# Halving the raw weight tiles and doubling the width of their splits in a two-block transformer kernel

## The chip, the core and the metric

The kernel runs on one core of a Trainium2 chip. Its time is the device time of one execution in microseconds (us), from the first to the last instruction. Six names are used for the engines: PE is TensorE's matrix products, PEld its loads of stationary operands, DVE is VectorE, ACT is ScalarE, POOL is GpSimd, and SP is SyncE, which here does nothing but issue transfers. An engine takes its instructions strictly in the order in which the build has placed them; an instruction that waits holds up all that stand behind it on that engine.

## What is computed

The reference takes 256 tokens of width 1024 through two blocks in float32. Cut to what matters here:

```
x = x + concat(mla, fox, chunk attention) @ w_o       # block 1
x = x + cross attention over a memory of 256 tokens
x = x + (silu(h @ w_gate) * (h @ w_up)) @ w_down
for l in 0, 1:                                        # block 2
    x = x + gate_l * mixer_l(norm(x) * (1 + s_l) + b_l)
    h = norm(x) * (1 + s'_l) + b'_l
    16 experts of 16384 for each head and token (8 heads), by top-k of two lists of 128 keys
    x = x + gate'_l * sum over the chosen experts of softmax gate * gelu(u_e . h) * v_e
```

The modulation rows s, b and gate are themselves products of a vector of 1024 with a matrix of 1024 x 12288. The sum over experts is computed densely: the kernel forms gelu(u . h) for all 16384 experts and all 256 tokens, multiplies by a map G of gates that is zero wherever an expert was not chosen, and multiplies that by all of v. So u and v (64 MB each, for each of two layers) stream through the core once.

## The kernel before, in words

Every product with a weight matrix keeps float32 accuracy by splitting both operands into two float32r parts, high and low, and summing three products: high by high, high by low, low by high. For weights the split is done on the fly, by two operations for each piece: ACT copies the raw weights to `wh` in float32r (L281), and DVE subtracts it from the raw weights to give `wl` (L282). A raw weight tile is 128 x 2048 floats, 1 MB, loaded by one transfer on SP's queue (`load_w`, L274, and L1574 for v) into a ring `wraw` of 3 tiles. The split tiles are 128 x 512, in a ring of 5 for `wh` and 5 for `wl`. So each raw tile is split by four pairs of operations.

Four helpers use these tiles. `feat` (L324) makes 256 features of (h @ W) transposed, with 48 products of 256 columns for each raw tile (L298 to L300). `proj` (L339) makes 512 columns of h @ W token-major (L287 to L291). `wide_mm` (L372) multiplies a chunk of 128 rows with all 1024 columns (L379), and `wide_end` (L381) does the last two chunks of such a sum.

Each layer of block 2 passes over the experts twice. The first pass runs `feat` over u for 64 pairs of expert rows and writes gelu(u . h) to DRAM (`act`). The second pass runs `wide_mm` over v, also for 64 pairs: for pair n, `gated(n)` reads `act` back (L1523, into a tile `k2` of a ring of 5 that also holds its product), multiplies it by the map of gates on DVE (L1525), and splits the product into the high part on ACT (L1532) and the low part on DVE (L1533). Then two calls of `wide_mm` give 24 products of 512 columns.

In the second pass of layer 0 another stream runs beside it: the modulation of the other layer. For most pairs SP also loads 512 KB of its matrix (L435) and DVE multiplies and sums it in one operation of 128 x 1024 (L436). In layer 1 nothing runs beside the second pass.

The order of instructions on each engine is set at build time by a scheduler that weighs priorities and readiness; the order of rings and waits follows from it. On SP's queue the loads of v, of the modulation's matrix and of `act` stand in one line, so a load that waits for a buffer holds up the ones behind it.

Of the kernel before, what the change touches and what calls it, by code (L numbers as in the profile page):

```python
# [19 lines left out]
P = 128  # L20
# [13 lines left out]
# the candidate pairs of two descending lists of 16: rows from..to, columns, place of the first  # L34
# [6 lines left out]
# the reciprocal root's first guess, its first step y (C - x y^2) K, and what weighs its second  # L41
# [4 lines left out]
# columns of the per-partition constants, in the order kernel() lays them out  # L46
# [12 lines left out]
# shape-only constants: name -> width of its [128, width] block  # L59
# [14 lines left out]
def body(tc, A, out, dbg=None, stop=None):  # L74
# [17 lines left out]
    wp = pool("wraw", 3)  # L92
    sp = pool("split", 5)
# [81 lines left out]
    def inv_rms(dst, s0, s1, e=D * EPS):  # L175
        """dst [128, 1] = 1/sqrt((s0 + s1 + e) / 1024) (each [128, 1])."""
# [5 lines left out]
    def inv_rms_w(dst, s0, width):  # L182
        """dst [128, 1] = 1/sqrt(s0 / width + EPS)."""
# [5 lines left out]
    def diag(r):  # L189
        """[128, 128] with r [128, 1] on the diagonal: a transpose through it scales its rows."""  # L190
# [4 lines left out]
    def hl_tiles(kc, pl=None, name="hl"):  # L195
        """feature-major operand [128, kc, 256] as exact float32r parts, in pieces of 4 chunks."""
# [13 lines left out]
    def split_psum(hl, k, src, gain=None, bias=None, scale=None):  # L210
        """chunk(s) k of hl from src (PSUM [128, n, 256]); per-partition gain/bias columns."""
# [24 lines left out]
    def to_T(src, kc, hl, gain=None, bias=None, by=None, ks=None):  # L236
        """src(t, k) -> [128 tok, 128] AP; transposed (with rows scaled by the diagonals by[t]), scaled and split into hl."""
# [32 lines left out]
    def load_w(dram, off, per, ada=True):  # L270
        """one raw weight tile: [128, per] floats, contiguous by partition."""
        ada_tick(ada)
        w = wp.tile([P, 2048], F32, name="w")
        nc.sync.dma_start(w[:, :per], dap(dram, off, [[per, P], [1, per]]))  # L274
        return w

    def split_w(src, n):
        """float32r parts of src [128, n <= 512]."""
        h = sp.tile([P, 512], F32R, name="wh")
        l = sp.tile([P, 512], F32R, name="wl")  # L280
        ada_p["act"] = nc.scalar.activation(h[:, :n], src, AF.Copy).ins.name  # L281
        i_ = nc.vector.tensor_sub(l[:, :n], src, h[:, :n].bitcast(F32))  # L282
        ada_p["after"] = i_.ins.name
# [11 lines left out]
    def mmT(ps, hl, k, wh, wl, start, stop):  # L295
        """ps [features, 256] += W[k]^T @ chunk k of hl"""
# [5 lines left out]
    # work that runs beside a stream of weights, in portions between its pieces  # L302
# [33 lines left out]
    def proj(hl, kc, dram, off, n, evac, base=0, quiet=0, turn=None):  # L336
        """[256 tok, n <= 512] = hl^T @ W, W at dram[off] as pieces [128, 4 chunks, n]."""
# [9 lines left out]
        for k in order:  # L347
            m = min(4, kc - k)
            w = load_w(dram, off + k * P * n, m * n, len(order) - order.index(k) > quiet)
            j = 0  # L350
            while j < m:
                # the last two chunks tile by tile, so that the first tile's end comes early
                final = k == order[-1]
                js = [j, j + 1] if final and j == m - 2 else [j]
                if final and turn:
                    js = [turn[i] for i in js]
                ws = [split_w(w[:, q * n:(q + 1) * n], n) for q in js]
                last = None
                for t in range(2):
                    sl = slice(t * P, (t + 1) * P)  # L360
                    for q, (wh, wl) in zip(js, ws):
                        h_, l_ = pick(base + k + q, sl)
                        i_ = mm3(ps[t][:, :n], h_, l_, wh[:, :n], wl[:, :n], k == order[0] and j == 0 and q == js[0],
                                 final and j + len(js) == m and q == js[-1], after=last)
                        last = i_.ins.name if len(js) == 2 else None
                    if final and j + len(js) == m:
                        evac(t, ps[t][:, :n])
                for _ in js:
                    tick()
                j += len(js)  # L370

    def wide_mm(ps, w, i, lhs_of, first, last):  # L372
        """ps[t, half] += lhs_of(t)^T @ w[:, i*1024...]"""
        wh, wl = zip(*(split_w(w[:, i * 1024 + hf * 512:i * 1024 + (hf + 1) * 512], 512) for hf in range(2)))
        for t in range(2):
            h, l = lhs_of(t)
            for lhs, ww in ((h, wh), (h, wl), (l, wh)):
                for hf in range(2):
                    nc.tensor.matmul(ps[t, hf], lhs, ww[hf], start=first and lhs is h and ww is wh, stop=last and lhs is l)  # L379

    def wide_end(ps, w, lhs_of, evac):  # L381
        """the last pair of chunks, tile by tile and half by half"""
        ws = [[split_w(w[:, i * 1024 + hf * 512:i * 1024 + (hf + 1) * 512], 512) for i in range(2)] for hf in range(2)]
        last = None
        for t in range(2):
            for hf in range(2):
                for i in range(2):
                    last = mm3(ps[t, hf], *lhs_of(i, t), *ws[hf][i], False, i == 1, after=last).ins.name
# [1384 lines left out]
```

## Time and profile before

| what | value |
|---|---|
| time, median of 3 runs | 2292.16 us (2290.60 to 2295.77) |
| span of the profiled execution, first to last instruction | 2295.8 us |
| the slowest of the three runs, which agrees with that span | 2295.77 us |
| PE busy | 2259.0 us, 98% |
| DVE busy | 1753.4 us, 76% |
| ACT busy | 1274.5 us, 56% |
| transfers, mean over the span | 219 GB/s |

The profiled execution has nothing around its span that the times would add: its span equals the time of the slowest run. It lies 3.6 us above the median.

Busy time of PE is to be read with care: products are pipelined, and a product that is shown for 390 ns may follow the one before after 226 ns. How fast PE goes is therefore read from the number of products in a stretch, not from its busy share.

### The profile page before, as it was taken

What the parts mean: (1) busy time and instruction counts of PE and PEld (TensorE: products, weight loads), DVE (VectorE), ACT (ScalarE), POOL (GpSimd) and SP (SyncE); (2) the same over time, 40 slices, a digit from 0 to 9 for tenths busy, and PEclk for the clock granted to TensorE, in tenths of its full rate; (3) what the DMA queues carried; (4) which work ended last, traced back from release to release, by engine and by line L of the source; (5) the groups of instructions that cost most, each with busy time, mean ns of one, the idle gap of its engine ahead of it and who ended that gap; (6) DMA issues with size and microseconds to landing.
All of it is one profiled execution on the core that took longest, in us unless ns stands there. A gap on an engine that the chain in (4) does not pass through costs nothing.

```text
span 2295.8 us, 40651 instructions
## 1 busy us (share of the span) xinstructions
PE 2259.0 (98%) x15032; PEld 2053.3 (89%) x15032; DVE 1753.4 (76%) x4239; ACT 1274.5 (56%) x2324; POOL 20.6 (1%) x28
## 2 busy tenths in 40 slices
PE   8999999999999999999999999999999999999998
PEld 7889988899999999887778877999999999888886
DVE  7778887798767675688888888896767665777776
ACT  7656555455455555555555565555555555555554
POOL 0000000000000000000000020000000000000000
PEclk9999999999999999999999999999999999999999
DMA  6256786446655555889889533456555557666664
GB/s 249 97 183 249 275 317 236 168 166 234 212 180 175 183 183 185 289 313 322 318 314 325 209 129 134 169 207 222 192 184 174 175 181 248 252 252 237 245 245 145
DMA packets 107161, 503.59 MB, mean 219 GB/s; under 512 B 12369, under 2 KB 13521, under 8 KB 61650
## 3 DMA queue, kind: packets, MB, share of 16 engines
q1 hardware_dynamic: 87954, 465.19, 57.9%
q10 hardware_dynamic: 18720, 33.72, 3.9%
q8 instruction: 117, 1.92, 0.3%
q0 software_dynamic: 288, 2.10, 0.2%
q14 instruction: 82, 0.67, 0.1%
HBM read 464.25 MB, written 36.70 MB: 218 GB/s over the span
## 4 chain that ended last, share of the span: by engine, by line
PE 85%; DVE 7%; DMA 5%; ACT 1%; issue 1%; DVEq 0%; SPq 0%; ACTq 0%
PE acc L379 21%; PE acc L298 14%; PE acc L299 14%; PE acc L300 14%; DMA k<-act 5%; PE acc L287 4%; PE acc L290 3%; PE acc L291 3%; DVE wl L282 3%; PE mm L1491 3%; PE mm L1492 3%; DVE G L436 1%; PE pt L246 1%; PE pt L300 1%; PE pt L299 1%
## 5 line engine op out<-in xcount | busy, mean ns | idle before, releaser
L281 ACT ACTIVATE wh<-w 128x512 fp32r<-128x512 f32 (+1 forms) x1408 | 882.2, 630 | 847.7 <-PE acc L299 383.9
L282 DVE TENSOR_TENSOR wl<-w,wh 128x512 fp32r<-128x512 f32 (+1 forms) x1408 | 954.7, 689 | 283.1 <-ACT wh L281 275.2
L298 PE MATMUL acc<-q,wh 128*128 128x256 f32 x2592 | 745.2, 288 | 0.7 <-ACT q L223 0.7
L299 PE MATMUL acc<-q,wh 128*128 128x256 f32 x2592 | 733.2, 283 | 0.5 <-DVE q L224 0.5
L300 PE MATMUL acc<-q,wl 128*128 128x256 f32 x2592 | 729.8, 283 | 1.2 <-DVE wl L282 1.2
L379 PE MATMUL acc<-wh,q 128*128 128x512 f32 x1984 | 612.1, 390 | 0.0
L298 PEld LDWEIGHTS acc<-q,wh 128*128 128x128 f32 x2592 | 497.9, 192 | 1.5 <-ACT q L223 0.9
L299 PEld LDWEIGHTS acc<-q,wh 128*128 128x128 f32 x2592 | 497.2, 192 | 0.8 <-DVE q L224 0.7
L300 PEld LDWEIGHTS acc<-q,wl 128*128 128x128 f32 x2592 | 495.7, 192 | 1.4 <-DVE wl L282 1.4
L379 PEld LDWEIGHTS acc<-wh,q 128*128 128x128 f32 x1984 | 373.0, 188 | 77.1
L379 PE MATMUL acc<-wl,q 128*128 128x512 f32 x992 | 388.1, 393 | 7.0 <-DVE wl L282 6.7
L379 PEld LDWEIGHTS acc<-wl,q 128*128 128x128 f32 x992 | 186.6, 188 | 52.3 <-DVE wl L282 14.1
L1478 DVE TENSOR_TENSOR ohe<-iota,ijh 128x512 f16<-128x512 f16 x128 | 54.1, 425 | 121.3 <-PE mm L1492 121.3
L1525 DVE SCALAR_TENSOR_TENSOR k<-k,G 128x512 f32<-128x512 f32 x128 | 88.2, 689 | 65.2 <-DMA k<-act 63.8
L1492 PE MATMUL mm<-ohe,k 128*128 128x128 f16 x512 | 128.0, 297 | 0.0
L1491 PE MATMUL mm<-k 128*128 128x128 f16 x512 | 126.6, 293 | 0.0
L1493 ACT ACTIVATE G<-mm 128x512 f32<-128x512 f32 x128 | 76.5, 598 | 38.0 <-PE mm L1492 38.0
L290 PE MATMUL acc<-wl,q 128*128 128x512 f32 (+1 forms) x224 | 89.8, 402 | 0.0
L291 PE MATMUL acc<-wh,q 128*128 128x512 f32 (+1 forms) x224 | 87.1, 397 | 0.0
L1533 DVE TENSOR_TENSOR q<-k,q 128x512 fp32r<-128x512 f32 x126 | 86.2, 684 | 0.7
L287 PE MATMUL acc<-wh,q 128*128 128x512 f32 (+1 forms) x224 | 85.3, 402 | 0.0
L1532 ACT ACTIVATE q<-k 128x512 fp32r<-128x512 f32 x126 | 77.8, 617 | 11.6 <-DVE k L1525 11.4
(458 smaller groups left out, 2316.4 us busy)
## 6 DMA issues: line engine op xcount, KB each, us to landing
w<-in_peer_u_dram SPq DMA_DIRECT2D x128, 1024.0 KB, 5.3
w<-in_peer_v_dram SPq DMA_DIRECT2D x128, 1024.0 KB, 4.9
act<-k ACTq DMA_DIRECT2D x128, 256.0 KB, 4.7
k<-act SPq DMA_DIRECT2D x128, 256.0 KB, 5.3
G<-in_ada_w_dram SPq DMA_DIRECT2D x52, 512.0 KB, 7.3
w<-in_w_gu_dram SPq DMA_DIRECT2D x22, 1024.0 KB, 4.9
adw<-in_ada_w_dram SPq DMA_DIRECT2D x44, 512.0 KB, 5.5
w<-in_peer_w_q_dram SPq DMA_DIRECT2D x16, 1024.0 KB, 4.7
```

The lines of the kernel that those rows point to most:

```text
L281: ada_p["act"] = nc.scalar.activation(h[:, :n], src, AF.Copy).ins.name
L282: i_ = nc.vector.tensor_sub(l[:, :n], src, h[:, :n].bitcast(F32))
L287: i_ = nc.tensor.matmul(ps, lh, wh, start=start, stop=False)
L290: nc.tensor.matmul(ps, lh, wl, start=False, stop=False)
L291: i_ = nc.tensor.matmul(ps, ll, wh, start=False, stop=stop)
L298: nc.tensor.matmul(ps, wh, h, start=start, stop=False)
L299: nc.tensor.matmul(ps, wh, l, start=False, stop=False)
L300: nc.tensor.matmul(ps, wl, h, start=False, stop=stop)
L379: nc.tensor.matmul(ps[t, hf], lhs, ww[hf], start=first and lhs is h and ww is wh, stop=last and lhs is l)
L1491: nc.tensor.matmul(pg[:, i, :], a[:, :, i], b[:, :, i], start=True, stop=False)
L1492: nc.tensor.matmul(pg[:, i, :], a[:, :, i], e[:, :, i], start=False, stop=True)
L1525: nc.vector.scalar_tensor_tensor(wt, ag, 1.0 / GATE, G[0][:, 2 * n:2 * n + 2, :], op0=OP.mult, op1=OP.mult)
```

## The change

Raw tiles become 128 x 1024 (512 KB) in a ring of 5, and split tiles 128 x 1024 in a ring of 3 for each part. `split_w` takes one or more sources and fills one pair of split tiles; with one source of 1024 columns it is one operation of ACT and one of DVE. Memory in the rings goes from 24 + 20 KB to 20 + 24 KB per partition. `feat` loads two halves instead of one tile; `proj` loads two chunks of 128 rows at a time instead of four; `wide` and the second pass over the experts load each chunk of 128 x 1024 by itself. Where the last two chunks are taken half by half (`wide_end`), the two split tiles are filled by two operations of 512 columns for each part, as many as before. At the end of the second pass the row of gates and the final gain get one raw tile each, and the old x comes into two tiles of the ring `q4`, no longer into the raw ring. Comments of the file are left out by the change, which moves its line numbers: L281 and L282 become L284 and L285, L379 becomes L384, L435 and L436 become L442 and L443, L1523, L1525, L1532 and L1533 become L1530, L1532, L1539 and L1540.

```diff
-    wp = pool("wraw", 3)
-    sp = pool("split", 5)
+    wp = pool("wraw", 5)
+    sp = pool("split", 3)
...
-    def load_w(dram, off, per, ada=True):
-        ada_tick(ada)
-        w = wp.tile([P, 2048], F32, name="w")
-        nc.sync.dma_start(w[:, :per], dap(dram, off, [[per, P], [1, per]]))
+    def load_w(dram, off, per, n):
+        w = wp.tile([P, 1024], F32, name="w")
+        nc.sync.dma_start(w[:, :n], dap(dram, off, [[per, P], [1, n]]))
         return w
-    def split_w(src, n):
-        h = sp.tile([P, 512], F32R, name="wh")
-        l = sp.tile([P, 512], F32R, name="wl")
-        ada_p["act"] = nc.scalar.activation(h[:, :n], src, AF.Copy).ins.name
-        i_ = nc.vector.tensor_sub(l[:, :n], src, h[:, :n].bitcast(F32))
-        ada_p["after"] = i_.ins.name
+    def split_w(*srcs):
+        h = sp.tile([P, 1024], F32R, name="wh")
+        l = sp.tile([P, 1024], F32R, name="wl")
+        c = 0
+        for src in srcs:
+            sl = slice(c, c + src.shape[-1])
+            c = sl.stop
+            ada_p["act"] = nc.scalar.activation(h[:, sl], src, AF.Copy).ins.name
+            i_ = nc.vector.tensor_sub(l[:, sl], src, h[:, sl].bitcast(F32))
+            ada_p["after"] = i_.ins.name
         return h, l
...
     # feat
-        w = load_w(dram, off, 2048)
+        ada_tick()
-        for q in range(4):
-            wh, wl = split_w(w[:, q * 512:(q + 1) * 512], 512)
-            for i in range(4):
-                k = (q % 2) * 4 + i
-                mmT(acc[:, q // 2, :], hl, k, wh[:, i * P:(i + 1) * P], wl[:, i * P:(i + 1) * P], k == 0, k == 7)
-            tick()
+        for q in range(2):
+            wh, wl = split_w(load_w(dram, off + q * 1024, 2048, 1024))
+            for k in range(8):
+                mmT(acc[:, q, :], hl, k, wh[:, k * P:(k + 1) * P], wl[:, k * P:(k + 1) * P], k == 0, k == 7)
+                if k % 4 == 3:
+                    tick()
...
-    def wide_mm(ps, w, i, lhs_of, first, last):
-        wh, wl = zip(*(split_w(w[:, i * 1024 + hf * 512:i * 1024 + (hf + 1) * 512], 512) for hf in range(2)))
+    def wide_mm(ps, w, lhs_of, first, last):
+        wh, wl = split_w(w)
...
     # second pass over the experts
-            w = wp.tile([P, 2048], F32, name="w")
-            nc.sync.dma_start(w, dap(A["peer_v_2"], l * 16384 * 1024 + n * 2048, [[P * 1024, P], [1, 2048]]))
+            w = [load_w(A["peer_v_2"], l * 16384 * 1024 + n * 2048 + i * 1024, P * 1024, 1024) for i in range(2)]
```

What this does to the order shows best in the second pass of layer 0. On DVE, before, `k2` is the tile of the ring of 5, `q4` the split gate products, `w`, `wh` and `wl` the weights, `G` the modulation's piece; the numbers tell tiles apart:

```order
L1533 TENSOR_TENSOR q4_13037<-k2_13035,q4_13037 128x512
L282 TENSOR_TENSOR wl_12943<-w_12929,wh_12942 128x512
L1525 SCALAR_TENSOR_TENSOR k2_13189<-k2_13187,G_7868 128x512
L282 TENSOR_TENSOR wl_12959<-w_12929,wh_12958 128x512
L282 TENSOR_TENSOR wl_12963<-w_12929,wh_12962 128x512
L436 SCALAR_TENSOR_TENSOR G_7868,mod_86<-G_7868 128x1024
L282 TENSOR_TENSOR wl_12990<-w_12980,wh_12989 128x512
L1533 TENSOR_TENSOR q4_13089<-k2_13087,q4_13089 128x512
L1525 SCALAR_TENSOR_TENSOR k2_13240<-k2_13238,G_7868 128x512
```

On DVE now, in the same place of the same pass:

```order
L1532 SCALAR_TENSOR_TENSOR k2_12333<-k2_12331,G_7322 128x512
L285 TENSOR_TENSOR wl_12113<-w_12101,wh_12112 128x1024
L1540 TENSOR_TENSOR q4_12200<-k2_12198,q4_12200 128x512
L285 TENSOR_TENSOR wl_12129<-w_12103,wh_12128 128x1024
L443 SCALAR_TENSOR_TENSOR G_7322,mod_86<-G_7322 128x1024
L1532 SCALAR_TENSOR_TENSOR k2_12378<-k2_12376,G_7322 128x512
```

For each pair four splits of 512 columns have become two of 1024. The order around them has moved too: the product with the gates (L1532, before L1525) now follows the modulation's operation, and the split of an older product (L1540, before L1533) stands between the two splits, not next to L1532. On SP's queue, before, one pair is three loads (v, the modulation's matrix, `act`):

```order
L1574 DMA w_12980<-in_peer_v_2_dram 128x2048
L435 DMA G_7868<-in_ada_w_2_dram 128x1024
L1523 DMA k2_13187<-act0_22_8212 128x512
L1574 DMA w_13031<-in_peer_v_2_dram 128x2048
L435 DMA G_7868<-in_ada_w_2_dram 128x1024
L1523 DMA k2_13238<-act0_23_8310 128x512
```

On SP's queue now, one pair is four loads:

```order
L1530 DMA k2_12331<-act0_24_7831 128x512
L273 DMA w_12149<-in_peer_v_2_dram 128x1024
L273 DMA w_12192<-in_peer_v_2_dram 128x1024
L442 DMA G_7322<-in_ada_w_2_dram 128x1024
L1530 DMA k2_12376<-act0_25_7928 128x512
L273 DMA w_12194<-in_peer_v_2_dram 128x1024
```

The load of `act` keeps its place behind the modulation's, but what it waits for has changed with the ring's new phase: in the built program before, the load of `k2_13238` waits until L1533 has read the product of four pairs earlier (`q4_13037`, the first row above); in the built program now, the load of `k2_12376` waits until L1532 of the pair before (`k2_12333`, the first row of its piece) has read its own input.

## Rows read from the trace of the kernel before

**Rows 1.** Page, part 1: busy us, share of the span, instructions.
```profile
PE 2259.0 (98%) x15032; PEld 2053.3 (89%) x15032; DVE 1753.4 (76%) x4239; ACT 1274.5 (56%) x2324; POOL 20.6 (1%) x28
```
**Rows 2.** Chain that ended last, by line, layer 0's second pass (940:1300).
```profile
by line: PE acc L379 35.3%; DMA k<-act 31.9%; DVE wl L282 14.7%; DVE G L436 5.8%; issue 3.8%; DVE q L1533 3.4%; DVE k L1525 2.2%; DMA w<-in_od_w_in_dram 1.3%; ACT wh L281 0.7%; PE mm L410 0.4%; ACT L430 0.3%; ACT G L430 0.3%; SPq L1574 0.3%
```
**Rows 3.** The same chain, layer 1's second pass (2000:2200).
```profile
by line: PE acc L379 100.1%
```
**Rows 4.** Windows: stretch, us, busy by engine (instructions), clock, DMA share, GB/s.
```profile
515.00:940.00 425.00, 425.00 (x3581) 421.28 (x3580) 299.34 (x783) 229.02 (x381) 0.00 (x0) 1.00 0.59 196
...
980.00:1260.00 280.00, 273.28 (x1179) 220.82 (x1178) 236.34 (x397) 151.74 (x249) 0.00 (x0) 0.99 0.90 319
...
1980.00:2260.00 280.00, 280.00 (x1239) 231.86 (x1238) 205.44 (x317) 156.44 (x258) 0.00 (x0) 1.00 0.67 241
```
**Rows 5.** Waits, 980:1260: engine, line, waited for: us, times, longest.
```profile
DVE k L1525 <- DMA k<-act: 43.1, 37, 3.4
PEld acc L379 <- DVE wl L282: 13.4, 17, 2.5
```
**Rows 6.** Chain in order of time, 1100:1126: start us, us, what.
```profile
1103.20 0.61 DVE q L1533
...
1103.83 6.70 DMA k<-act
...
1110.62 0.24 DVE k L1525
...
1111.23 1.89 DVE wl L282 x3
1113.12 1.14 DVE G L436 x2
...
1115.49 7.14 DMA k<-act
```
**Rows 7.** Timeline of SP's queue, layer 0: start, us, line, what.
```profile
1106.37 0.33 SPq L1574 DMA_DIRECT2D w<-in_peer_v_dram  x1
1107.51 0.33 SPq L435 DMA_DIRECT2D G<-in_ada_w_dram  x1
1108.72 0.33 SPq L1523 DMA_DIRECT2D k<-act  x1
```
**Rows 8.** Loads of 1050:1200: what, count, KB, us to landing (median).
```profile
w<-in_peer_v_dram SPq DMA_DIRECT2D x25, 1024.0 KB, 7.1
G<-in_ada_w_dram SPq DMA_DIRECT2D x25, 512.0 KB, 7.3
k<-act SPq DMA_DIRECT2D x26, 256.0 KB, 6.7
```
**Rows 9.** The same for layer 1, 2000:2200.
```profile
w<-in_peer_v_dram SPq DMA_DIRECT2D x37, 1024.0 KB, 4.7
k<-act SPq DMA_DIRECT2D x38, 256.0 KB, 3.1
```
**Rows 10.** SP's waits in 1980:2260: line, waited for: us, times, longest.
```profile
SPq L1523 <- DVE k L1525: 95.3, 46, 2.9
```
**Rows 11.** DVE's waits in 1980:2260, the same columns.
```profile
DVE k L1525 <- DMA k<-act: 8.0, 7, 3.3
```
**Rows 12.** Timeline of SP's queue, layer 1.
```profile
2055.79 0.33 SPq L1574 DMA_DIRECT2D w<-in_peer_v_dram  x1
2058.02 0.32 SPq L1523 DMA_DIRECT2D k<-act  x1
```
**Rows 13.** Groups by form, whole span: count | busy us, mean ns | idle before.
```profile
L282 DVE TENSOR_TENSOR wl<-w,wh 128x512 fp32r<-128x512 f32 x1397 | 948.6, 690 | 282.7 <-ACT wh L281 275.0 <-PE acc L299 0.6
L281 ACT ACTIVATE wh<-w 128x512 fp32r<-128x512 f32 x1397 | 876.8, 631 | 846.1 <-PE acc L299 383.9 <-PE acc L379 253.4 <-DVE wl L282 76.1
L436 DVE SCALAR_TENSOR_TENSOR G<-G 128x1024 f32<-128x1024 f32 x52 | 63.3, 1217 | 0.0
L430 ACT ACTIVATE G<-G 128x1024 f32<-128x1024 f32 x1 | 1.1, 1062 | 0.0
```
**Rows 14.** The chain that ended last, by line, whole span.
```profile
by line: PE acc L379 21.3%; PE acc L298 13.8%; PE acc L299 13.8%; PE acc L300 13.7%; DMA k<-act 5.0%; PE acc L287 3.5%; PE acc L290 3.5%; PE acc L291 3.5%; DVE wl L282 2.9%; PE mm L1491 2.6%; PE mm L1492 2.6%; DVE G L436 0.9%; issue 0.9%; P
```

More of the change, by code (lines that the diff above doesn't have):

```diff
@@ L324, in feat, with proj @@
     def feat(hl, dram, off, evac, late=False):
[L326 removed]
+        ada_tick()
         acc = ptr.tile([P, 2, S], F32, name="pt") if late else pacc.tile([P, 2, S], F32, name="acc")
[L328 to L333 removed]
+        for q in range(2):
[4 more added lines that the diff above has]
+                    tick()
         evac(acc)
[L336 removed]
+    def proj(hl, kc, dram, off, n, evac, base=0, quiet=0, turned=False):
         def pick(kk, sl):
@@ L348, in proj @@
             m = min(4, kc - k)
[L349 to L357, printed above, removed]
-                last = None
[L359 to L370, printed above, removed]
@@ L372, in wide_mm @@
-    def wide_mm(ps, w, i, lhs_of, first, last):
-        wh, wl = zip(*(split_w(w[:, i * 1024 + hf * 512:i * 1024 + (hf + 1) * 512], 512) for hf in range(2)))
+            ada_tick(len(order) - order.index(k) > quiet)
+            js = list(range(0, m, 2))
+            if k == order[-1] and turned:
+                js.reverse()
+            for j in js:
+                c = min(2, m - j)
+                wh, wl = split_w(load_w(dram, off + k * P * n + j * n, m * n, c * n)[:, :c * n])
+                final = k == order[-1] and j == js[-1]
+                last = None
+                for q, t in [(q, t) for t in range(2) for q in range(c)] if final else [(q, t) for q in range(c) for t in range(2)]:
+                    h_, l_ = pick(base + k + j + q, slice(t * P, (t + 1) * P))
+                    cs = slice(q * n, (q + 1) * n)
+                    i_ = mm3(ps[t][:, :n], h_, l_, wh[:, cs], wl[:, cs], k == order[0] and j == js[0] and q == 0,
+                             final and q == c - 1, after=last)
+                    if final:
+                        last = i_.ins.name
+                        if q == c - 1:
+                            evac(t, ps[t][:, :n])
+                    elif t:
+                        tick()
+                if final:
+                    for _ in range(c):
+                        tick()
@@ L378, in wide_mm @@
                 for hf in range(2):
-                    nc.tensor.matmul(ps[t, hf], lhs, ww[hf], start=first and lhs is h and ww is wh, stop=last and lhs is l)
+                    nc.tensor.matmul(ps[t, hf], lhs, ww[:, hf * 512:(hf + 1) * 512], start=first and lhs is h and ww is wh, stop=last and lhs is l)
     def wide_end(ps, w, lhs_of, evac):
-        ws = [[split_w(w[:, i * 1024 + hf * 512:i * 1024 + (hf + 1) * 512], 512) for i in range(2)] for hf in range(2)]
+        ws = [split_w(*(w[i][:, hf * 512:(hf + 1) * 512] for i in range(2))) for hf in range(2)]
         last = None
@@ L387, in wide_end @@
                 for i in range(2):
-                    last = mm3(ps[t, hf], *lhs_of(i, t), *ws[hf][i], False, i == 1, after=last).ins.name
+                    wh, wl = (z[:, i * 512:(i + 1) * 512] for z in ws[hf])
+                    last = mm3(ps[t, hf], *lhs_of(i, t), wh, wl, False, i == 1, after=last).ins.name
                 evac(hf)(t, ps[t, hf])
@@ L393, in wide @@
         for k in range(k0, k1, 2):
-            w = load_w(dram, k * P * 1024, 2048, k + 2 < nk)
+            ada_tick(k + 2 < nk)
+            w = [load_w(dram, k * P * 1024 + i * 1024, 2048, 1024) for i in range(2)]
             if k + 2 < nk:
                 for i in range(2):
-                    wide_mm(ps, w, i, lambda t: pick(k + i, slice(t * P, (t + 1) * P)), k + i == 0, False)
+                    wide_mm(ps, w[i], lambda t: pick(k + i, slice(t * P, (t + 1) * P)), k + i == 0, False)
                     tick()
@@ L778, in body @@
     c_hl = hl_tiles(8, cp, "xh")
-    proj(hl, 8, A["w_o"], 0, 512, add_x(0), turn=(2, 3, 0, 1))
+    proj(hl, 8, A["w_o"], 0, 512, add_x(0), turned=True)
     for k in (0, 2):
@@ L782, in body @@
     pace["rate"], pace["due"] = 0.3, 0.0
-    proj(hl, 8, A["w_o"], 1024 * 512, 512, add_x(1), turn=(2, 3, 0, 1))
+    proj(hl, 8, A["w_o"], 1024 * 512, 512, add_x(1), turned=True)
     side_done()
@@ L1577, in peer @@
                 for i in range(2):
-                    wide_mm(ps, w, i, lambda t: (wh_[:, i, t * P:(t + 1) * P], wl_[:, i, t * P:(t + 1) * P]),
+                    wide_mm(ps, w[i], lambda t: (wh_[:, i, t * P:(t + 1) * P], wl_[:, i, t * P:(t + 1) * P]),
                             n == 0 and i == 0, False)
                 continue
-            rows_ = wp.tile([P, 2048], F32, name="w")
-            xo = wp.tile([P, 2048], F32, name="w")
-            nc.sync.dma_start(xo, xd)
+            grow = wp.tile([P, D], F32, name="w")
+            xo = []
+            for t in range(2):
+                xo.append(q4.tile([P, D], F32, name="q4"))
+                nc.sync.dma_start(xo[t], xd[:, t * D:(t + 1) * D])
             if l == 1:
-                nc.sync.dma_start(rows_[:, D:2 * D], dap(A["final_norm_2"], 0, [[0, P], [1, D]]))
+                frow = wp.tile([P, D], F32, name="w")
+                nc.sync.dma_start(frow, dap(A["final_norm_2"], 0, [[0, P], [1, D]]))
             ones = st.tile([P, 512], F32, name="k2", bufs=NK2)[:, 0:P]
             nc.vector.memset(ones, 1.0)
-            g_row(rows_[:, 0:D], ones, mod[:, l, 40:48])
+            g_row(grow, ones, mod[:, l, 40:48])
             ps0.close()
@@ L1598, in f @@
                 def f(t, acc):
-                    nc.vector.tensor_mul(xn[:, t, hs], acc, rows_[:, hs])
-                    nc.vector.tensor_add(xn[:, t, hs], xn[:, t, hs], xo[:, t * D + hf * 512:t * D + (hf + 1) * 512])
+                    nc.vector.tensor_mul(xn[:, t, hs], acc, grow[:, hs])
+                    nc.vector.tensor_add(xn[:, t, hs], xn[:, t, hs], xo[t][:, hs])
                     part_sq(ss, xn, t, hf, "a")
@@ L1605, in peer @@
         if l == 1:
-            return xn, ss, ns, rows_[:, D:2 * D]
+            return xn, ss, ns, frow
         keep_warm(WARM[2])
```

## The prediction

> **What bounds the kernel now.** I first read the busy shares: PE has 98%, its weight loads 89%, and the other engines 76% and less [rows 1]. Products are pipelined, so the share alone does not say that PE goes at its own pace; I therefore took the chain that ended last by stage, and then counted products in windows. In the second pass over the experts of layer 1 the chain is PE alone [rows 3], and 1239 products start in 280 us: 0.226 us each, 5.42 us for the 24 of one pair [rows 4]. The first pass is also without a gap on PE, and its clock is full [rows 4]. In these stages a shorter split is worth nothing. The second pass of layer 0 is different: in the same 280 us only 1179 products start, so a pair takes 5.70 us, and the 60 missing products are 60 x 0.226 = 13.6 us [rows 4]. Its chain runs a third through the read of `act` and a quarter through DVE [rows 2]. DVE waits 43.1 us for that read there, and PE then waits for `wl` [rows 5].
>
> The chain in order of time shows the loop. L1533 ends, SP issues the read at 1103.83, it lands 6.70 us later, L1525 uses it, and DVE goes through three splits, the modulation's operation, another split and L1533, before the read after next is issued at 1115.49: 11.66 us for two pairs, 5.83 each [rows 6]. The read is that slow because 1 MB of v and 512 KB of the modulation go out 2.35 and 1.21 us before it on the same queue [rows 7], and all three land about 7 us after issue [rows 8], with the transfers 90% busy [rows 4]. In layer 1, with no modulation beside it, the read lands after 3.1 us [rows 9].
>
> **The splits themselves.** A split of 512 columns takes 631 ns on ACT and 690 ns on DVE; operations of 1024 columns take 1062 and 1217 ns [rows 13]. I take these for the new splits. They take the place of 1397 each [rows 13], so ACT's busy time falls by about 698 x 0.20 = 140 us and DVE's by 698 x 0.16 = 114 us. Neither is on the path where PE is the chain, and PE's work hides all of it: this is worth 0, except in the pass of layer 0.
>
> **The pass of layer 0.** DVE's work for a pair, by starts one after another: three splits take 1.89 - 0.08 = 1.81 us, so 0.60 each, the modulation 1.14 and L1533 0.61 [rows 6], L1525 about as much as L1533. Before: 4 x 0.60 + 1.14 + 0.61 + 0.61 = 4.77. Now two splits of about 1.14: 2 x 1.14 + 1.14 + 0.61 + 0.61 = 4.64. That is below PE's 5.42 either way, so what decides is the wait for the read. The new order ties each read to L1532 of the pair before it (L1525 in the old numbers), and the read is needed by the next L1532. So the loop goes once around per pair: landing + 0.65 for the operation + 0.05 to the issue. It fits into 5.42 if the read lands within 4.7 us.
>
> Layer 1 has that very wait in its trace: SP waits 95.3 us for L1525, 46 times [rows 10], the read lands in 3.1 us [rows 9], and DVE waits for it only 7 times, for 8.0 us [rows 11]. What differs in layer 0 is the modulation's load just before the read. I estimate its cost from landings. With the medians, v issued at 1106.37 lands at 1113.5, 3.0 us after the read of 1103.83 (1110.5); the modulation's load lands at 1114.8, 1.3 us later; the next read at 1115.4, 0.6 us later [rows 6 to 8]. So the queue needs 3.0 + 1.3 + 0.6 = 4.9 us for a pair, which is less than 5.42. In layer 1 v goes out 2.23 us before the read [rows 12], is through at 0.8, the read at 1.4, and lands at 3.1: 1.7 us stay for what is not queueing. Now the new order in a pair of 5.42 us: the halves of v go out when the splits free their tiles, 4.2 and 2.5 us before the read, the modulation's load 1.3 before. They are through at -2.7, -1.0 and 0.3, the read at 0.9, so it lands at 2.6 us. The same count for the old order gives 4.25 us, where the trace has 6.7, so it runs up to 2.4 us low; with that, 5.0. Between 2.6 and 5.0 I take 3.8, nearer to layer 1's 3.1 because the wait is the same one: it fits under 4.7. The pass then goes at PE's pace but for a few late reads. Taking layer 1's 8.0 us of waits at the old exchange of 13.6 us lost for 43.1 waited, 2.5 us stay lost: gain 13.6 - 2.5 = 11.1 us. The bounds are 13.6 gained, and with 5.0 us a pair of 5.70, which is no gain at all.
>
> **One more load per pair.** The same bytes now go in four loads, two of them with rows of 4 KB and not 8. I cost this at 0: the modulation's 512 KB with rows of 4 KB took 1.3 us where 1 MB took 3.0. The cover is 5.42 - 4.9 = 0.5 us, or a quarter of a microsecond for each half of v.
>
> The Trainium skill, on its page "DMA: Bandwidth & Descriptors", section "Bandwidth", advises transfers of at least 1 MiB, and its section "Anatomy of one DMA — SWDGE (gpsimd) path" puts a fixed cost of about 2.0 us on each. If that cost occupied the queue, an estimate from that page is 4.9 + 2.0 = 6.9 us for a pair, some 59 us more over 49 pairs. The landings above, 1.3 and 0.6 us apart, speak against it.
>
> **Starts of stages.** DVE's split is on the chain outside this pass too: 2.9% of 2295.8 us less 14.7% of the 360 us of rows 2, so 66.6 - 52.9 = 13.7 us, about 20 links of 0.69 [rows 2, 13, 14]. Where such a link is the latency of a first split, it grows by 1.22 - 0.69 = 0.53 us, and ACT's before it by 1.06 - 0.63 = 0.43: at most 20 x 0.96 = 19 us more. Where it is only DVE being full, it shrinks by 1.14 for 1.20, some 0.7 us in all; and the wait for the odd mixer's first weights (1.3% of 360 us, 4.7 us, rows 2) may go as well, so the other bound is 5 us less. Weights do not depend on the norms, and the ring holds 3 x 1024 columns of them ahead at a start instead of 5 x 512, so most starts hide the longer split: I take +2.5 us.
>
> **Sum.** 2295.8 - 11.1 + 2.5 = 2287.2 us for the profiled execution, which has no time around its span. It lies 3.6 us above the median, so the forecast for the median is 2292.2 - 8.6 = 2283.6 us.
>
> **The rivals.**
>
> The gain is not there, because the reads stay late or the queue sets the pace. For it: the transfers are 90% busy in this pass, and my count of landings ran 2.4 us low in the old order. Against it: 4.9 us of transfers for a pair. At 5.0 us of landing the pair stays at 5.70, and with the starts' 0 to 2.5 us the time is 2292 to 2295.
>
> The once-around loop is slower than the old one. The old order gave each read two pairs in which to come round; the new one gives it one. If the read kept landing at 6.7 us, the pair would take 6.7 + 0.70 = 7.4 us, 1.7 more than now, and 49 pairs 83 us more: 2375. It is slower from 5.0 us of landing on, and each 0.1 us beyond costs 4.9 us. Against the full price: a longer pair empties the queue, so the landing falls back towards layer 1's. I give it 2297 to 2375, with 2310 as its middle.
>
> The longer first splits cost more than the pass returns: all 20 links at their full 0.96 us give -11.1 + 19 = +8, so 2300; half of them 2291. Against it: over the whole span the two links together, DVE's and ACT's, would all have to be latencies, and the chain outside the pass names DVE's splits for 13.7 of some 1936 us only [rows 14].
>
> Everything goes well: 13.6 gained, and up to 3 at the starts: 2276 to 2279.
>
> **How the numbers follow.** Forecast 0.50, with a range of its own of 2279 to 2288.5; no gain 0.21; the slower loop 0.10; the starts 0.13; all well 0.06. Less than 0.2%, 4.6 us, cannot be told from no change by these runs: faster means below 2287.6, slower above 2296.7. Faster: 0.45 of the forecast's 0.50, and 0.06, and 0.01 of the starts, makes 0.52. Slower: 0.10, 0.08 of the starts and 0.02 each from the tails of the first two, 0.22. The same: 0.26. The range is 2276 to 2306: it leaves out most of the slow loop and the tail of the best case.
>
> **What would show it.** In the pass of layer 0: 49 pairs in some 267 us, the window's products near 1239 for 280 us, the read landing below 4.7 us, and DVE's wait for it well below 43 us. ACT's splits near 1.06 us and DVE's near 1.22. In the first pass and in layer 1 the same pitch of PE as now. If the pass still shows 1180 products in 280 us, the first rival holds; if fewer, the second; if the pass gained and the time did not, PE must show new gaps before the first products of stages. The prediction is wrong if the difference comes from the first pass or from layer 1's second pass, where I see nothing to gain or lose.

## The result, and the profile after

The changed kernel takes 2316.4 us (median of four runs, 2311.9 to 2322.2) against 2292.4 for the kernel before: 1.0106 times as long, 95% interval 1.0084 to 1.0128. The forecast was 2283.6, with 2306 as the upper end of its range: the change makes the kernel slower, and the prediction was wrong. A later series, beside the experiments, gave 2312.5 against 2297.7, 1.0065 [1.0052, 1.0078]; one slow execution of it, 3111.0 us at a granted clock of 0.65, is left out. The two ratios do not agree within their intervals. The execution profiled here took 2311.87 us, its span 2310.0, against 2295.8 before; the executions near 2321 us were not profiled, and what they lose beyond this one has no account here.

The first part of the page answers to [rows 1]: DVE and ACT are less busy, by 71 and 130 us, and PE is busy 9 us longer.

```profile
PE 2267.8 (98%) x15032; PEld 2058.1 (89%) x15032; DVE 1682.4 (73%) x3542; ACT 1144.2 (50%) x1627; POOL 25.1 (1%) x28
```

The groups by form answer to [rows 13], with count, busy time and mean ns. The splits cost what was forecast (1217 and 1062 ns), and there are half as many.

```profile
L285 DVE TENSOR_TENSOR wl<-w,wh 128x1024 fp32r<-128x1024 f32 x692 | 847.1, 1225 | 354.2 <-ACT wh L284 353.6
L284 ACT ACTIVATE wh<-w 128x1024 fp32r<-128x1024 f32 x692 | 733.5, 1060 | 916.5 <-PE acc L302 412.7 <-PE acc L384 337.8 <-PE acc L294 77.7
```

The windows answer to [rows 4]; a fourth, 1944:2010, holds the start of layer 1's second pass. The last row is the kernel before in that window.

```profile
515.00:940.00 425.00, 425.00 (x3580) 421.15 (x3580) 289.89 (x691) 202.63 (x256) 0.00 (x0) 1.00 0.60 193
980.00:1260.00 280.00, 275.61 (x1198) 223.08 (x1197) 232.00 (x302) 134.83 (x153) 0.00 (x0) 1.00 0.93 324
1944.00:2010.00 66.00, 62.11 (x263) 49.90 (x262) 44.88 (x52) 30.33 (x37) 0.00 (x0) 0.97 0.77 247
1980.00:2260.00 280.00, 278.14 (x1224) 229.31 (x1224) 194.24 (x210) 134.73 (x153) 0.00 (x0) 1.00 0.76 243
```
```profile
1944.00:2010.00 66.00, 66.00 (x292) 54.63 (x292) 49.70 (x81) 37.87 (x65) 0.00 (x0) 1.00 0.71 259
```

The first pass is unchanged. The second pass of layer 0 has 19 products more in its window (4.3 us at 0.226), where 60 were wanted. Layer 1's second pass has lost some 29 of 292 at its start. In layer 0 DVE still waits for the read of `act`; these waits in 980:1260 answer to [rows 5]. SP now waits 24 times for one read's landing before it issues another; in the kernel before it has no such wait in this window.

```profile
DVE k L1532 <- DMA k<-act: 47.8, 38, 2.4
PEld acc L384 <- DVE wl L285: 10.8, 18, 1.2
```
```profile
SPq L1530 <- DMA k<-act: 26.4, 24, 1.9
SPq L1530 <- DVE k L1532: 23.4, 39, 0.8
```

The windows hold 280 us of each pass, and most of the loss lies outside them. I followed it by the start of one instruction per stage (the first and last start that the view of a source line gives). The table has the time in the kernel before, and how much later, in us, each kernel comes there; e1 to e10 are the experiments below, and line numbers are the changed kernel's.

| reached | before | changed | e1 pieces | e2 raw | e8 units | e5 follow | e10 coarse | e9 all | e6 before |
|---|---|---|---|---|---|---|---|---|---|
| FFN's first gate, L913 | 187.5 | +4.7 | +1.9 | -1.3 | +0.7 | +4.5 | +5.0 | -0.8 | 0.0 |
| even mixer, L1066 first | 411.3 | +9.7 | +4.7 | +4.7 | +5.7 | +9.3 | +9.4 | -1.0 | +0.1 |
| first gelu, L1549 | 514.0 | +10.1 | +5.5 | +4.6 | +5.7 | +9.7 | +8.1 | -1.0 | +0.1 |
| first of the last gelus, layer 0 | 924.5 | +10.3 | +5.8 | +4.7 | +5.8 | +10.0 | +8.4 | -1.0 | +0.2 |
| odd mixer, L1184 first | 1334.3 | +8.1 | +4.9 | -1.8 | -2.6 | -1.0 | -3.5 | -14.8 | -12.6 |
| last gelu, layer 1 | 1936.0 | +8.0 | +5.0 | -1.7 | -4.1 | -1.1 | -3.6 | -16.3 | -12.5 |
| the end, L1642 last | 2291.8 | +14.3 | +10.5 | +1.0 | -2.5 | +0.5 | -2.2 | -15.3 | -11.5 |

Each column is one execution. Two executions of the changed kernel differ by 1.9 us at the first gelu and by 5.5 at layer 1's last gelu, so a difference of 2 us between two columns shows nothing by itself.

So the changed kernel loses 4.7 us by the FFN, 5.0 from there to the even mixer and 6.3 in layer 1's second pass, and wins 2.2 in layer 0's second pass. Its second profile has the same losses (+4.9 by the FFN, 5.8 in layer 1) but a gain of 5.7 in layer 0.

**By the FFN.** In the changed kernel's order on DVE a split of 1024 columns stands in front of the last softmax product of the cross attention (`s`, L825), and that product now comes behind the evacuation `vx` (L856), which needs the projection's last products. In the kernel before, `s` stood ahead of `vx`, and the splits between were half as long. The timeline of DVE, the changed kernel first, then the kernel before: start us, us, what.

```profile
155.61 1.22 DVE L285 TENSOR_TENSOR wl<-w,wh 128x1024 fp32r<-128x1024 f32 x1
156.75 0.16 DVE L824 RECIPROCAL nx<-nx 128x2 f32<-128x2 f32 x1
156.82 0.73 DVE L856 TENSOR_SCALAR vx<-acc,rm 128x512 f32<-128x512 f32 x1
157.47 0.68 DVE L825 TENSOR_TENSOR s<-s,nx 128x512 f32<-128x512 f32 x1
```
```profile
154.65 0.69 DVE L818 TENSOR_TENSOR s<-s,nx 128x512 f32<-128x512 f32 x1
155.26 0.69 DVE L282 TENSOR_TENSOR wl<-w,wh 128x512 fp32r<-128x512 f32 x1
156.44 0.75 DVE L849 TENSOR_SCALAR vx<-acc,rm 128x512 f32<-128x512 f32 x1 [0.49 <-PE acc L291]
```

PE's timeline shows the price: it stands 1.29 us for `s`, and then sixteen products take 5.41 us; in the kernel before (last row) they take 3.72.

```profile
158.21 0.66 PE L833 MATMUL pt<-ck,s 128*128 128x128 f32 x4 [1.29 <-DVE s L825]
159.33 5.41 PE L867 MATMUL pt<-sT,vx 128*128 128x256 f32 x16 [0.47 <-ACT sT L839]
```
```profile
157.74 3.72 PE L860 MATMUL pt<-sT,vx 128*128 128x256 f32 x16 [0.47 <-ACT sT L832]
```

The granted clock of that stretch is 0.69 of full speed; in the kernel before it is 1.00.

```profile
160.00:165.00 5.00, 5.00 (x17) 4.14 (x16) 0.69 (x1) 0.82 (x2) 0.00 (x0) 0.69 0.29 107
```

The product behind the sixteen starts 3.3 us late (164.39 against 161.11). The other 1.4 of the 4.7 us come between there and L913; the granted clock falls once more on that way, to 0.66 in 180:185 (1.00 in the kernel before); what makes it fall there was not tried.

**Layer 1's second pass.** PE stands here at two places; the kernel before has no wait of PE in this window. PE's waits in 1944:2010:

```profile
PE acc L384 <- ACT q L1539: 2.0, 1, 2.0
PE acc L384 <- DVE wl L285: 1.8, 2, 1.1
```

The first is one stand of 2.03 us, at 1950.62, for the product of pair 1, whose read of `act` SP issued only at 1942.94, behind four loads of `v`. The granted clock is 0.72 in 1950:1956. Pair 1 so starts 2.2 us behind PE's pace, and its first 16 products take 5.4 us where 3.6 are the pace: about 4.0 of the 6.3 us. The second place is 1980:1992, with 42 products where 53 fit, about 2.5 us. In the second profile it is the other way round: the first stand is 1.12 us, and 1966:1986 has 69 products where 88 fit.

What leads to the second place begins earlier, while PE still goes without a gap. The chain of waits from 1958.95 on (start us, us, what): the gate's operation on DVE, a split, SP's issue of the `v` load that the split lets go, the read of `act` that stands behind it on SP, and the next split behind that read's own operation (L1532, at 1965.35 on DVE, here under "issue").

```profile
1958.95 0.69 DVE k L1532
1959.65 1.15 DVE wl L285
1960.81 0.33 SPq L273
1961.14 0.05 issue
1961.23 4.09 DMA k<-act
1965.38 0.08 issue
1965.48 0.47 issue
1965.95 1.23 DVE wl L285
```

From split to split this is 6.3 us, and in it DVE goes through two splits, which is one pair; PE needs 5.42, so the splits lose their lead until PE stands for `wl`. The order on DVE shows why: the gate's operation (L1532) of a later pair stands in front of each split. Between the first splits of pairs 2 and 7 it holds ten of them, until the operation is five pairs ahead of the splits; the kernel before has eight there.

### The profile page after: what moved, and what is told of

Read it like the earlier page. It is cut to its first block, busy times and chain, and to the rows that moved or that the text cites. A ratio compares the mean times of both kernels' runs of the same rounds, so it can differ in the third digit from the quotient of the medians.

```text
span 2310.0 us, 39164 instructions
## 1 busy us (share of the span) xinstructions
PE 2267.8 (98%) x15032; PEld 2058.1 (89%) x15032; DVE 1682.4 (73%) x3542; ACT 1144.2 (50%) x1627; POOL 25.1 (1%) x28
## 4 chain that ended last, share of the span: by engine, by line
PE 81%; DMA 10%; DVE 6%; issue 2%; ACT 1%; SPq 0%; DVEq 0%; ACTq 0%
PE acc L384 17%; PE acc L301 14%; PE acc L302 14%; PE acc L303 14%; DMA k<-act 8%; PE acc L293 4%; PE acc L290 4%; PE acc L294 4%; DVE wl L285 3%; PE mm L1498 3%; PE mm L1499 3%; DVE k L1532 1%; PE pt L246 1%; PE pt L302 1%; PE pt L301 1%
## 5 line engine op out<-in xcount | busy, mean ns | idle before, releaser
L284 ACT ACTIVATE wh<-w 128x1024 fp32r<-128x1024 f32 (+2 forms) x711 | 745.8, 1050 | 923.3 <-PE acc L302 412.7
L285 DVE TENSOR_TENSOR wl<-w,wh 128x1024 fp32r<-128x1024 f32 (+2 forms) x711 | 860.9, 1212 | 359.9 <-ACT wh L284 359.3
L384 PE MATMUL acc<-wh,q 128*128 128x512 f32 x1984 | 532.4, 390 | 3.8 <-ACT q L1539 3.8
L384 PEld LDWEIGHTS acc<-wh,q 128*128 128x128 f32 x1984 | 373.1, 188 | 83.3 <-ACT q L1539 4.7
L384 PE MATMUL acc<-wl,q 128*128 128x512 f32 x992 | 308.9, 393 | 6.2 <-DVE wl L285 6.0
L384 PEld LDWEIGHTS acc<-wl,q 128*128 128x128 f32 x992 | 183.9, 188 | 50.9 <-DVE wl L285 14.1
L1532 DVE SCALAR_TENSOR_TENSOR k<-k,G 128x512 f32<-128x512 f32 x128 | 88.6, 692 | 85.1 <-DMA k<-act 83.0
L1539 ACT ACTIVATE q<-k 128x512 fp32r<-128x512 f32 x126 | 77.6, 616 | 18.0 <-DVE k L1532 18.0
L1540 DVE TENSOR_TENSOR q<-k,q 128x512 fp32r<-128x512 f32 x126 | 86.2, 684 | 0.0
```

Source lines behind the costliest of these rows:

```text
L284: ada_p["act"] = nc.scalar.activation(h[:, sl], src, AF.Copy).ins.name
L285: i_ = nc.vector.tensor_sub(l[:, sl], src, h[:, sl].bitcast(F32))
L384: nc.tensor.matmul(ps[t, hf], lhs, ww[:, hf * 512:(hf + 1) * 512], start=first and lhs is h and ww is wh, stop=last and lhs is l)
L1532: nc.vector.scalar_tensor_tensor(wt, ag, 1.0 / GATE, G[0][:, 2 * n:2 * n + 2, :], op0=OP.mult, op1=OP.mult)
```

## The experiments

Each was timed beside the kernel before on the same chip (2297 us there), so kernels of different series are compared by their ratios to it; e9 to e11 ran together. Where an edit changes the program's order, I name what moved.

**e0_again**: the changed kernel, unedited.

> The changed kernel once more, for its spread. Its times so far fall in two groups, near 2311.9 and near 2321.5 us. If these are two courses of the same program, the times fall in the two groups again and a profile of the upper one shows where the 9.6 us arise; if it was chance, the times fill the range between. Either theory of the loss (long operations, or halved loads) expects 2312 to 2322.

Measured: 2312.5 us, ratio 1.0065 [1.0052, 1.0078]. The five times fill the range from 2305.8 to 2315.5: no two groups, and none near 2321. Layer 0's pass differs from execution to execution, as the two gains of 2.2 and 5.7 us show.

**e1_pieces**: only the length of the operations.

```
-        for src in srcs:
+        for src in [s_[:, a_:min(a_ + 512, s_.shape[-1])] for s_ in srcs for a_ in range(0, s_.shape[-1], 512)]:
```

> The changed kernel with its tiles, rings and loads, but each split made in operations of 512 columns again. Theory A, long operations: in front of a latency chain an operation of 1.05 or 1.21 us on ACT or DVE holds up what stands behind it, products stop and the clock falls; then the 10 us lost by the first gelu go (first gelu near 514 us, not 524) and the time is 2300 to 2306; the loss at the start of layer 1's second pass, 6 us, may stay. Theory B, halved loads: nothing changes, 2312 to 2322.

Measured: 2313.9 us, ratio 1.0070 [1.0056, 1.0083], the changed kernel's: in the time nothing comes back, and theory A's 2300 to 2306 failed. In the profiles 4.6 of the 10.1 us lost by the first gelu come back (519.5 us), 2.7 against the second profile, so theory A holds for a part of the starts. At the cross attention PE still stands 1.37 us for `s`, since the two pieces of a tile stand together, but the sixteen products behind it take 3.72 us: here the same wait did not cost the clock at once (in 175:180 it is 0.75). The passes keep their losses, 5.5 us in layer 1, and layer 0 wins only 0.9. The first stand in layer 1 is there too, 2.08 us.

**e2_raw**: only the loads (the kernel before; halves of each raw tile loaded apart).

```
-    wp = pool("wraw", 3)
+    wp = pool("wraw", 5)
-        w = wp.tile([P, 2048], F32, name="w")
+                w = wp.tile([P, 1024], F32, name="w")
```

> The kernel before with raw tiles of 128x1024 in a ring of 5, each of its loads cut in two; splits stay at 512 columns in a ring of 5. Theory A, long operations: the stages up to the first gelu stay as before (first gelu near 514 us), 2290 to 2298. Theory B, halved loads and their order on SP: the loss is all here, 2308 to 2320, with the first gelu near 524 us and 264 products in the first 66 us of layer 1's second pass.

Measured: 2298.2 us, ratio 1.0001 [0.9991, 1.0011]. Theory B falls: halved loads cost nothing in sum. But the sum hides two things. Layer 0's pass wins 6.5 us, and the even mixer's start loses 6.0. There the new order puts the product of `wsT` and `tri` ahead of the first evacuation of the transposes (L233), and DVE stands until `tri`, the last of six loads that SP issues there, has landed:

```profile
370.80 0.15 DVE L173 SCALAR_TENSOR_TENSOR r__4584<-rs_v 128x1 f32<-128x1 f32 x1
375.49 0.90 DVE L1052 TENSOR_TENSOR wsT<-wsT,tri 128x128 f32<-128x128 f32 x4 [4.54 <-DMA tri<-in_cst_dram]
376.30 0.48 DVE L233 SCALAR_TENSOR_TENSOR k<-pt,a,q 128x256 f32<-128x256 f32 x1
```

**e4_inplace**: the changed kernel; one tile a pair, so reads run five pairs ahead.

```
-            wt = st.tile([P, 2, S], F32, name="k2", bufs=NK2)
+            wt = ag
```

> The changed kernel with one edit in the second pass: the gated activations are written over the read of act, so that a pair takes one k2 tile and not two, and the read of a pair waits for the pair five before it, no longer for the one before. Theory C, the read of act on a loop of one pair: the waits of DVE for the read (61 us in layer 0) go, 980 to 1260 us holds some 1239 products and layer 1's start some 292 in 66 us, so 9 + 6 us are won: 2296 to 2307. If DVE's or the transfers' load sets the pace there, nothing changes in layer 0 (1198 products) and at most the 6 us of layer 1 are won: 2306 to 2316.

Measured: 2390.5 us, ratio 1.0400 [1.0382, 1.0417]. Theory C fails as I put it: deeper reads made the second passes of the two layers 42 and 49 us slower than in the kernel before. The tile of read X is released by the `wl` of pair X-5 (L1540), and the gate's operation of pair X stands on DVE only one split behind that release. DVE is in order, so it stands until the read that was just issued lands. The timeline of DVE in layer 1:

```profile
2101.74 0.69 DVE L1532 SCALAR_TENSOR_TENSOR k<-k,G 128x512 f32<-128x512 f32 x1 [2.54 <-DMA k<-act]
2102.35 1.22 DVE L285 TENSOR_TENSOR wl<-w,wh 128x1024 fp32r<-128x1024 f32 x1
2103.48 0.69 DVE L1540 TENSOR_TENSOR q<-k,q 128x512 fp32r<-128x512 f32 x1
2104.08 1.22 DVE L285 TENSOR_TENSOR wl<-w,wh 128x1024 fp32r<-128x1024 f32 x1
2107.98 0.69 DVE L1532 SCALAR_TENSOR_TENSOR k<-k,G 128x512 f32<-128x512 f32 x1 [2.68 <-DMA k<-act]
```

A pair takes 6.24 us, the release, the landing (3.8 us from SP's issue at 2104.20) and what stands between. The depth of the ring is spent by the place of one instruction. This gave a new form of theory C: with one tile a pair, the place of the gate's operation decides.

**e5_follow** (changed kernel) and **e6_before_follow** (kernel before): in place as in e4, and the gate's operation held back.

```
-            nc.vector.scalar_tensor_tensor(wt, ag, 1.0 / GATE, ...)
+            i_ = nc.vector.scalar_tensor_tensor(wt, ag, 1.0 / GATE, ...)
+            if len(ends) >= 2:
+                follow(i_, ends[-2])
...
+                ends.append(ada_p["after"])
```

> The changed kernel with the gated activations written over the read of act (reads five pairs ahead) and the gate's operation held behind the splits of the pair two before on DVE. Theory C, the place of the gate's operation: in the run without this hold the operation stood one split behind the release of its own read and DVE waited 75 us; here it stands some 18 us behind its read, so DVE's waits for act are near 0, 980 to 1260 us holds some 1239 products and 1944 to 2010 us some 292. That wins 9 + 6 us on the changed kernel: 2296 to 2306 on this scale, 2313.8 less 8 to 18. If it is the transfers or DVE's load that set the pace, layer 0 stays near 1200 products and the time near 2312.

> The kernel before with the same two edits in the second pass (written over, and held). Its second pass over layer 0 loses 13.6 us to the read of act and layer 1's none. Theory C: 13 us less than before, ratio 0.994, with some 1239 products in 980 to 1260 us. If the transfers set the pace (their busy share is 0.90 there): less than 4 us.

Measured: e5 2298.1 us, ratio 1.0004 [0.9994, 1.0013]; e6 2283.8 us, ratio 0.9943 [0.9930, 0.9956], faster than both kernels. Both held. In e5 DVE has no wait for the read left in 980:1260, although the reads land later than before (5.2 us after issue, 4.4 in the changed kernel), and the transfers' share is 0.95. The windows, e5 first:

```profile
980.00:1260.00 280.00, 280.00 (x1238) 231.82 (x1236) 240.23 (x311) 144.23 (x157) 0.00 (x0) 1.00 0.95 333
1944.00:2010.00 66.00, 66.00 (x293) 54.67 (x292) 45.72 (x52) 32.54 (x38) 0.00 (x0) 1.00 0.77 258
```
```profile
980.00:1260.00 280.00, 280.00 (x1237) 231.90 (x1236) 252.10 (x418) 154.06 (x260) 0.00 (x0) 1.00 0.93 332
1980.00:2260.00 280.00, 280.00 (x1238) 231.94 (x1237) 206.01 (x315) 161.72 (x256) 0.00 (x0) 1.00 0.64 238
```

Neither the transfers nor DVE's load set the pace of layer 0's pass, in either kernel. In layer 1 the hold takes the second place of standing away, not the first: e5's window begins behind it, and PE stands 1.85 us for pair 1 at 1941.29, though the clock stays at 1.00 there. The hold without the single tile was not tried. e5 at 1.0004 is 14 us better than e0_again at 1.0065; its 9.7 us by the first gelu stay, as nothing there was edited.

**e7_ws**: e2_raw with `wsT`'s products held behind the last split of the first projection.

```
-            nc.vector.tensor_mul(wsT[:, g, :], wsT[:, g, :], tri)
+            i_ = nc.vector.tensor_mul(wsT[:, g, :], wsT[:, g, :], tri)
+            follow(i_, ada_p["after"])
```

> The kernel before with halved loads (as e2_raw), and wsT's four products with tri held behind the last split of the even mixer's first projection on DVE. In e2_raw they stood ahead of the first evacuation of the transposes and waited 4.54 us for the landing of tri, TensorE stood 3.6 us and its clock fell. Theory D, a small load's landing put in front of a latency chain: that wait is gone, the even mixer's first products start 4 to 6 us earlier (416.0 us becomes 410 to 412) and the time is 4 to 6 us below e2_raw's: ratio 0.997 to 0.999. If the wait only hides another: no change against e2_raw.

Measured: 2293.8 us, ratio 0.9980 [0.9968, 0.9991]; the even mixer's L1066 starts at 410.2 us, 5.8 earlier than in e2_raw. Held.

**e8_units**: the changed kernel with split tiles of 512 columns as units of their own.

```
-    sp = pool("split", 3)
+    sp = pool("split", 5)
-        h = sp.tile([P, 1024], F32R, name="wh")
+            h = sp.tile([P, 512], F32R, name="wh")
```

> The changed kernel with split tiles of 512 columns (ring of 5) as units of their own, and all else of the change: halved loads, ring of 5 raw tiles, its order of code. Theory E, the coarse unit: a split of 1024 columns is one block for the order on ACT and DVE, and the last softmax product of the cross attention falls behind the evacuation there; with units of 512 DVE's order there is as before, and the time is that of e2_raw, 2294 to 2302 (ratio 0.999 to 1.003), with the FFN's first gate at 187 +-1.5 us. Theory F, the changed order of code (loads and ticks): as the changed kernel, ratio 1.006, gate near 192 us.

Measured: 2299.2 us, ratio 1.0013 [1.0002, 1.0023]; gate at 188.2 us. Theory E held. On DVE `s` stands ahead of `vx` again, and PE does not stand in front of the transposes:

```profile
155.50 1.03 PE L844 MATMUL pt<-ck,s 128*128 128x128 f32 x8
157.00 3.72 PE L878 MATMUL pt<-sT,vx 128*128 128x256 f32 x16 [0.47 <-ACT sT L850]
```

Units of 512 bring the second passes back as well, without any hold: from the first of layer 0's last gelus to the odd mixer e8 takes 401.4 us (changed kernel 407.6, before 409.8), and from layer 1's last gelu to the end 357.4 (362.1, and 355.8), which is e5's 357.4. The stand of PE for the product of pair 1 is in all seven profiles with split tiles of 1024 columns (1.1 to 2.1 us) and in none of the six with 512.

**e9_all**: e8 with the edits of e5 and e7. **e10_coarse**: the changed kernel, coarse units kept, with the edits of e5 and e7. **e11_warm**: e10 with one number changed.

```
-WARM = 80, 80, 80, 80
+WARM = 120, 80, 80, 80
```

> The changed kernel with all three causes taken away: split tiles of 512 columns as units of their own, the gate's operation held behind the splits of the pair two before with reads five pairs ahead, and wsT's products held behind the first projection's last split. If these are the causes, the halved loads and the ring of 5 that remain cost nothing, and the time is that of e6_before_follow within 4 us: 2280 to 2288, ratio 0.993 to 0.996, with the first gelu within 1.5 us of the kernel before's 514.0. If there is a cost of the halved loads left over, it is 2289 or more.

> As e9_all but with the changed kernel's splits of 1024 columns. What it takes more than e9_all is the price of the coarse unit by itself at the starts of stages: 4.9 us at the cross attention and 2 to 5 at the even mixer, so 2288 to 2295 where e9_all has 2280 to 2288; first gelu at 520 to 523 us. If the coarse unit cost only through the waits that were taken away, e10 is within 2 us of e9_all.

> As e10_coarse with 120 and not 80 products for nothing ahead of the even mixer, to fill the 2.9 us in which TensorE stands there. If the loss there is the clock that falls after it (0.91 in 370 to 390 us), the clock is 1.00 there, and 1 to 2 us are won by the even mixer's first products (L1066) against e10_coarse; if it is only the wait for dg, nothing changes.

Measured: e9 2285.5 us, ratio 0.9949 [0.9935, 0.9963]; e10 2296.6, ratio 1.0000 [0.9991, 1.0009]; e11 2295.6, ratio 0.9989 [0.9980, 0.9998]. In e9 all that the change had lost is gone, and halved loads cost nothing that shows against e6. What e10 has more than e9, 11.1 us, is the coarse unit: the longer operation, the tile of 1024 and the ring of 3 for 5 together. That is more than the 7 to 10 I expected. In the profiles 9.1 us of it lie before the first gelu. A ring of 3 by itself was not tried. `wsT`'s hold did nothing for the even mixer's start here (L1066 at +9.4, in e5 +9.3). In e11 the 40 added products fill the gap: the first rows are e10's, the others e11's.

```profile
370.00:380.00 10.00, 7.10 (x94) 6.58 (x94) 8.36 (x49) 3.62 (x9) 0.00 (x0) 0.94 0.72 248
380.00:390.00 10.00, 10.00 (x53) 8.75 (x53) 7.71 (x17) 7.12 (x14) 0.00 (x0) 0.89 0.12 42
```
```profile
370.00:380.00 10.00, 9.33 (x139) 8.91 (x139) 8.06 (x50) 4.53 (x11) 0.00 (x0) 1.00 0.68 235
380.00:390.00 10.00, 10.00 (x53) 8.40 (x52) 9.16 (x24) 6.76 (x13) 0.00 (x0) 1.00 0.18 58
```

From L951 to L1066 e11 takes 45.4 us and e10 46.7: 1.3 us, as expected, for the clock. That is one profile of each; the times, 2295.6 and 2296.6, cannot be told apart.

## Why the prediction was wrong

Its sum was -11.1 for the pass of layer 0, +2.5 for the starts and 0 for the rest. The profiled execution has -2.2, +10.3 up to layer 0's last gelus, and +6.3 in layer 1's second pass; the second profile has -5.7, +8.4 and +5.8. All three terms failed.

- **The splits: right.** 1060 and 1225 ns; ACT fell by 130 us where 140 were forecast, DVE only by 71 where 114 were, and the first pass shows no time for it.
- **The step "layer 1's second pass, nothing to gain or lose" failed**, and I had named that as what would make the prediction wrong. I had looked at the steady part (1980:2260), where PE is the chain in the kernel before, and not at the pass's start, where the reads of `act` still have to get ahead. There PE stands for the late read of pair 1, and then the gate's operations crowd in front of the splits, each behind a read of 4 us. e5 takes the crowd away with the coarse unit and halved loads still there (1.6 us are left of 6.3); e8 takes both away by units of 512.
- **The starts of stages: mis-sized, +10.1 for +2.5.** "Most starts hide the longer split" was argued from the columns that the split ring holds ahead. The link that the trace shows paying at the cross attention is no first split: it is a softmax product behind a split on the same in-order engine. The rival with the long splits had the right sign, but its sum of +8 is short of the 14 us in the profile and the 24 in the time, and its price, the longer operation, is at most about half of the starts' loss (e1). The rest comes from the unit: with tiles of 512 as units e8 has the gate 4 us earlier, and e10 less e9 prices the coarse unit at 11.1 us.
- **The pass of layer 0: right place, landing mis-sized.** The forecast let the once-around loop run if the read landed within 4.7 us, and took 3.8 for every read. The median is 4.4, but the landings go from 3.6 to 6.2 us: the reads issued at 1096.99 and 1108.70 were waited for until 1103.36 and 1114.45 (stands of 2.38 and 1.69 us), the one between them not at all. So 47.8 us of waits stayed. Where the landing was near 4.5 us, the loop held the pace as forecast: in the second profile seven pairs from 1055.77 on take 5.33 us each, though DVE waits 0.4 to 0.7 us for every read. That a late read costs anything comes from the loop itself, where the next gate's operation follows its read at once: in e5 layer 0's reads land later (5.2 us) and the pair takes 5.42, while in e4, with the operation close behind the release, a pair of layer 1 takes 6.24 with a landing of 3.8.
- **One more load per pair at 0: right.** e2 has the ratio 1.0001, and e6 with whole loads and e9 with halves are alike (0.9943 and 0.9949), while the transfers' share in 1980:2260 rises from 0.64 to 0.71.

The Trainium skill, "DMA: Bandwidth & Descriptors", section "Bandwidth", advises transfers of at least 1 MiB. The rows agree that halves keep the transfers busier for the same bytes; no run here shows a time for it, and the 59 us that the prediction worked out from that page's fixed cost are not there.

Open is why the even mixer's start costs 3 us more with the coarse unit when neither `tri` nor the clock is late (e11, +3.1 from gate to L1066, of which 2.1 before the mixer's norm begins at L951); that the norm's chain on DVE starts late behind a split is seen in the trace, not tried. Open also is why the wait of 1.3 us at the cross attention is followed by a lower clock in the changed kernel and not in e1.

## What to carry to other kernels

A coarser operation that lowers an engine's busy time is worth nothing where that engine isn't the bound, and it can cost where a latency chain shares the in-order engine (11.1 us here): price it at the starts of stages and passes, not in their steady part. A deeper ring prefetches only as far as the in-order consumer lets it; look at where the consuming instruction stands in its engine's order, and hold it back. On the kernel before, one tile a pair together with the hold won 0.6%; the tile alone, in the changed kernel, lost over 3%. 130 us less of ACT won nothing. When an edit moves a scheduler's order, compare the order at each stage's start before trusting a sum of durations.

## What the runs showed of the hardware

Much the same wait of TensorE was followed by a lower clock or not: 1.29 us at 158.21 us was followed by 5.41 us for sixteen products, 1.37 us in e1 by 3.72. At the even mixer 40 products of no use cut a stand of 2.9 us to 0.7, and the granted clock behind it rose from 0.89 to 1.00 (1.3 us, one profile each). Reads of 256 KB landed in 3.6 to 6.2 us within one pass of the changed kernel. A median landing of 4.4 us went with 47.8 us of waits there, one of 5.2 us with none in e5.
